# Adaptive average pooling on one core: a partition owns 63 + 1 rows instead of 60 + 4

## The chip, the core and the metric

One core of a Trainium2 chip runs the kernel. The metric is the device time of one execution in microseconds (us); lower is better. The runs before the change took 333.34, 333.5 and 333.92 us, median 333.5.

## The reference

The input has 32 x 256 rows of 4096 float32 numbers, and each row is averaged in 256 windows of 16 neighbours:

```python
def reference(x, output_size):            # x: (32, 256, 4096) float32, output_size 256
    batch, channels, length = x.shape
    result = np.zeros((batch, channels, output_size), dtype=np.float32)
    for i in range(output_size):
        start = int(i * length / output_size)
        end = int((i + 1) * length / output_size)
        result[:, :, i] = np.mean(x[:, :, start:end], axis=-1)
    return result
```

134.22 MB are read and 8.39 MB written. A row is 16 KB of input and 1 KB of output, and there are 8192 rows, 64 for each of the 128 partitions.

## The kernel before

**Who owns which rows.** A tile is four rows for each partition, 64 KB of input per partition, and there are 16 tiles. The first 15 tiles come from one block: partition p owns the 60 neighbouring rows 60p to 60p+59, and tile t takes four of them. In DRAM the neighbouring partitions of such a tile read 960 KB apart. The last tile takes the last 512 rows of the input, four neighbouring rows for each partition, so its partitions read 64 KB apart.

**One tile.** SyncE issues the load of the tile into one of two buffers of the pool `inpool` (L75). The windows of a tile are split in two halves. On the second half GpSimd (POOL, L78) adds the upper eight elements of every window onto the lower eight. Meanwhile VectorE (DVE, L83) sums the windows of the first half, 16 elements each; then it sums the second half's eight (L86), which waits for GpSimd. ScalarE (ACT, L89) multiplies the results by 1/16 in place. The results of the first 15 tiles lie in `res_many`, 60 KB per partition, those of the last in `res_last`, 4 KB.

**Order.** The two buffers set the order: the load of tile t+2 is issued when VectorE has finished with tile t (L86), while the load of tile t+1 is moving. Before the second load VectorE writes 1536 zeros into its buffer (L74), and the load waits for that. All loads and stores are issued by SyncE, in program order, on one DMA queue.

**Stores.** The store of `res_many` stands right behind the last load in SyncE's program (L58 is the helper `store`). It waits until ScalarE has finished the fifteenth tile. When the last tile is done, two more stores follow, split by partition:

```python
    for lo, hi in ((0, 120), (120, P)):
        store(o_last[lo:hi, :], res_last[lo:hi, :])
```

The three stores count on one semaphore of their own, and SyncE waits for all of them at the end.

Of the kernel before, what the change touches and what calls it, by code (L numbers as in the profile page):

```python
# [1 line left out]

# [4 lines left out]


@with_exitstack
def kernel(  # L10
    ctx: ExitStack,
    tc: tile.TileContext,
    x: bass.AP,
    output_size: int,
    out: bass.AP,
):

    nc = tc.nc
    F32 = mybir.dt.float32
    X = mybir.AxisListType.X

    batch, channels, length = x.shape
    ob, oc, olen = out.shape
    assert ob == batch and oc == channels and olen == output_size
    assert length % output_size == 0
    window = length // output_size  # L30
    hw = window // 2
    inv_w = 1.0 / float(window)

    P = nc.NUM_PARTITIONS
    R = 4
    rows = batch * channels
    assert rows % (P * R) == 0
    ntiles = rows // (P * R)
    many = (ntiles - 1) * R
    cells = R * output_size  # L40
    m = cells // 2
    cols = R * length

    xr = x.rearrange("b c l -> (b c) l")
    orow = out.rearrange("b c o -> (b c) o")
    x_many = xr[0 : P * many, :].rearrange("(p r) l -> p (r l)", p=P, r=many)
    o_many = orow[0 : P * many, :].rearrange("(p r) o -> p (r o)", p=P, r=many)
    x_last = xr[P * many :, :].rearrange("(p r) l -> p (r l)", p=P, r=R)
    o_last = orow[P * many :, :].rearrange("(p r) o -> p (r o)", p=P, r=R)

    res_many = nc.alloc_sbuf_tensor("res_many", [P, (ntiles - 1) * cells], F32, align_bytes=256)
    res_last = nc.alloc_sbuf_tensor("res_last", [P, cells], F32, align_bytes=256)
    inpool = ctx.enter_context(tc.tile_pool(name="inpool", bufs=2))

    stored = nc.alloc_semaphore("stored")

    def store(out, in_):
        ins = nc.sync.dma_start(out=out, in_=in_)  # L58
        tc.no_tile_sem_insts.add(ins.ins.name)
        ins.then_inc(stored, 16)  # L60

    for t in range(ntiles):
        last = t == ntiles - 1
        xbuf = inpool.tile([P, cols + 64], F32, name="xin")
        off = 32 if last else 0
        flat = xbuf[:, off : off + cols]
        xin = flat.rearrange("p (o w) -> p o w", w=window)
        if last:
            res, base, src = res_last, 0, x_last
        else:  # L70
            res, base = res_many, t * cells
            src = x_many[:, t * cols : (t + 1) * cols]
        if t == 1:
            nc.vector.memset(flat[:, 0:1536], 0.0)  # L74
        nc.sync.dma_start(out=flat, in_=src)  # L75
        if last:
            store(o_many, res_many[:, :])
        nc.gpsimd.tensor_add(  # L78
            out=xin[:, m:cells, 0:hw],
            in0=xin[:, m:cells, 0:hw],  # L80
            in1=xin[:, m:cells, hw:window],
        )
        nc.vector.reduce_sum(  # L83
            out=res[:, base : base + m], in_=xin[:, 0:m, :], axis=X
        )
        nc.vector.reduce_sum(  # L86
            out=res[:, base + m : base + cells], in_=xin[:, m:cells, 0:hw], axis=X
        )
        nc.scalar.mul(  # L89
            out=res[:, base : base + cells],  # L90
            in_=res[:, base : base + cells],
            mul=inv_w,
        )
    for lo, hi in ((0, 120), (120, P)):
        store(o_last[lo:hi, :], res_last[lo:hi, :])

    ctx.pop_all().close()
    tc.close()
    tc.compile()  # L99
    nc.sync.wait_ge(stored, 48)  # L100
    nc.sync.sem_clear(stored)


# [1 line left out]
_INS = ['x', 'output_size']  # L105
_OUTS = [((32, 256, 256), 'float32')]

_NUMBERS = {'output_size': 256}


# [26 lines left out]
```

## Time and profile before

| what | us |
|---|---|
| device time, median of three runs (333.34 to 333.92) | 333.5 |
| span of the profiled execution, first to last instruction | 332.3 |
| the difference, time around the span | 1.2 |
| VectorE busy | 211.0 |
| GpSimd busy | 139.7 |
| ScalarE busy | 18.2 |
| one GpSimd addition of a tile (128x4096) | 8.72 |
| one VectorE sum of 16 (128x8192 to 128x512) | 8.69 |
| one VectorE sum of eight (128x4096 to 128x512) | 4.42 |
| one ScalarE multiplication (128x1024) | 1.06 |
| one load, time from landing to landing in the steady part | 19.3 |
| first load issued, landed | 0.74, 22.69 |

The profiled execution is known by its span; the time of the runs is taken without the profiler. A view "windows" cuts the span in stretches and gives for each the busy time of the engines, the share of time that the 16 DMA engines were busy, and the GB/s that they moved. A DMA packet is counted whole in the stretch where it starts, so in stretches shorter than a packet the share can exceed 1. "SPq" is SyncE's queue of instructions: a line with it says how long SyncE waited before it could issue a DMA.

### The profile page before, as it was taken

Reading aid. Unit: us, or ns where it says so; the run is one execution under the profiler, and the core shown is the slowest. Engines: PE = TensorE matmul, PEld = TensorE weight load, DVE = VectorE, ACT = ScalarE, POOL = GpSimd, SP = SyncE. Lnnn points to the kernel's source line nnn. Section 1 sums busy time; section 2 is a strip of 40 time slices with the busy share of each in tenths; the row PEclk is TensorE's granted clock in tenths of the full one; section 3 lists DMA queues with packets and bytes.
Section 4 is the critical chain, followed back from the end, with each engine's and each line's share of the span. In section 5 each row is a group of like instructions: output and inputs, shape, how many; then the busy total and the mean of one; then the engine's idle time right before and its main releaser. Section 6 shows DMA issues by size and latency. Waiting matters only on the chain.

```text
span 332.3 us, 162 instructions
## 1 busy us (share of the span) xinstructions
DVE 211.0 (64%) x33; ACT 18.2 (5%) x17; POOL 139.7 (42%) x20
## 2 busy tenths in 40 slices
DVE  1029396692939669392956939295683929578392
ACT  1000101001010100001010000101000010101001
POOL 0027091642709164370906437090633709063370
DMA  9898999989898999989898998989899898989897
GB/s 379 379 505 379 489 394 442 442 379 505 379 505 379 489 394 394 489 379 505 379 497 387 426 458 379 505 379 505 379 481 402 387 497 379 505 379 505 363 473 300
DMA packets 2599, 142.61 MB, mean 429 GB/s; under 512 B 295, under 2 KB 295, under 8 KB 423
## 3 DMA queue, kind: packets, MB, share of 16 engines
q1 hardware_dynamic: 2599, 142.61, 99.4%
HBM read 134.22 MB, written 8.39 MB: 429 GB/s over the span
## 4 chain that ended last, share of the span: by engine, by line
DMA 65%; POOL 18%; DVE 11%; POOLq 3%; issue 0%; ACT 0%
DMA xin<-in_x_dram 65%; POOL xin L78 18%; DVE res_many L86 9%; POOLq L99 3%; DVE res_last L86 1%; DVE xin L74 0%; ACT res_last L89 0%; POOLq L78 0%
## 5 line engine op out<-in xcount | busy, mean ns | idle before, releaser
L78 POOL TENSOR_TENSOR xin<-xin 128x4096 f32<-128x4096 f32 x16 | 139.5, 8717 | 181.9 <-DMA xin<-in_x_dram 181.9
L83 DVE TENSOR_REDUCE res_many<-xin 128x512 f32<-128x8192 f32 x15 | 130.3, 8686 | 105.0 <-DMA xin<-in_x_dram 105.0
L86 DVE TENSOR_REDUCE res_many<-xin 128x512 f32<-128x4096 f32 x15 | 66.3, 4420 | 2.4 <-POOL xin L78 2.3
L89 ACT ACTIVATE res_many<-res_many 128x1024 f32<-128x1024 f32 x15 | 15.8, 1056 | 289.7 <-DVE res_many L86 289.7
L83 DVE TENSOR_REDUCE res_last<-xin 128x512 f32<-128x8192 f32 x1 | 8.7, 8686 | 6.6 <-DMA xin<-in_x_dram 6.6
L86 DVE TENSOR_REDUCE res_last<-xin 128x512 f32<-128x4096 f32 x1 | 4.4, 4422 | 0.2 <-POOL xin L78 0.2
L89 ACT ACTIVATE res_last<-res_last 128x1024 f32<-128x1024 f32 x1 | 1.1, 1056 | 18.8 <-DVE res_last L86 18.8
L74 DVE MEMSET xin<- 128x1536 f32 x1 | 1.3, 1338 | 1.1 <-PEq L118 1.1
L89 ACT ACT_TABLE_LOAD x1 | 1.3, 1283 | 0.7 <-PEq L118 0.7
L118 POOL MEMSET const-float32-0.0<- 128x1 f32 x1 | 0.1, 98 | 0.2 <-issue 0.2
L118 POOL MEMSET const-bfloat16-1.0<- 128x1 bf16 x1 | 0.1, 101 | 0.0
L118 POOL MEMSET const-uint8-127<- 128x1 uint8 x1 | 0.1, 101 | 0.0
L118 POOL MEMSET const-float32-1.0<- 128x1 f32 x1 | 0.1, 98 | 0.0
## 6 DMA issues: line engine op xcount, KB each, us to landing
out_dram<-res_many SPq DMA_DIRECT2D x1, 7680.0 KB
out_dram<-res_last SPq DMA_DIRECT2D x1, 480.0 KB
xin<-in_x_dram SPq DMA_DIRECT2D x16, 25.3
out_dram<-res_last SPq DMA_DIRECT2D x1, 32.0 KB
```

What stands on the lines that cost most here:

```text
L74: nc.vector.memset(flat[:, 0:1536], 0.0)
L78: nc.gpsimd.tensor_add(out=xin[:, m:cells, 0:hw], in0=xin[:, m:cells, 0:hw], in1=xin[:, m:cells, hw:window],)
L83: nc.vector.reduce_sum(out=res[:, base : base + m], in_=xin[:, 0:m, :], axis=X)
L86: nc.vector.reduce_sum(out=res[:, base + m : base + cells], in_=xin[:, m:cells, 0:hw], axis=X)
L89: nc.scalar.mul(out=res[:, base : base + cells], in_=res[:, base : base + cells], mul=inv_w,)
L99: tc.compile()
L118: nc = _bacc.Bacc("TRN2", target_bir_lowering=False, num_devices=1)
```

## The change

A partition now owns 63 neighbouring rows of the block (rows 63p to 63p+62) and one of the last 128 rows. There are 17 loads: three rows, fifteen times four rows, and one row; the neighbouring partitions of the first 16 loads read 1008 KB apart, those of the last 16 KB apart. The results lie in three tensors: `res_many` (59 rows, 59 KB per partition), `res_late` (the last four of the 63, 4 KB) and `res_last` (one row, 1 KB), and each is stored by one DMA over all 128 partitions; the rows of the first two stores are 63 KB apart in DRAM. The split of the last store in 120 and 8 partitions is gone, and so is an offset of 32 elements that the last tile had in its buffer. The operations on a tile are the same, on three, four or one row. The last two loads are issued ahead of the store of `res_many` in SyncE's program, and that store waits for ScalarE's multiplication of the fifteenth load's tile.

```diff
-    ntiles = rows // (P * R)
-    many = (ntiles - 1) * R
-    cells = R * output_size
-    m = cells // 2
+    many = rows // P - 1
+    counts = [many % R] * (many % R > 0) + [R] * (many // R) + [1]
     cols = R * length
...
-    x_last = xr[P * many :, :].rearrange("(p r) l -> p (r l)", p=P, r=R)
-    o_last = orow[P * many :, :].rearrange("(p r) o -> p (r o)", p=P, r=R)
+    x_last = xr[P * many :, :]
+    o_last = orow[P * many :, :]
 
-    res_many = nc.alloc_sbuf_tensor("res_many", [P, (ntiles - 1) * cells], F32, align_bytes=256)
-    res_last = nc.alloc_sbuf_tensor("res_last", [P, cells], F32, align_bytes=256)
+    early = (many - R) * output_size
+    res_many = nc.alloc_sbuf_tensor("res_many", [P, early], F32, align_bytes=256)
+    res_late = nc.alloc_sbuf_tensor("res_late", [P, R * output_size], F32, align_bytes=256)
+    res_last = nc.alloc_sbuf_tensor("res_last", [P, output_size], F32, align_bytes=256)
...
+    def pooled(xin, res, n):
+        m = n // 2
+        nc.gpsimd.tensor_add(
+            out=xin[:, m:n, 0:hw], in0=xin[:, m:n, 0:hw], in1=xin[:, m:n, hw:window]
+        )
+        nc.vector.reduce_sum(out=res[:, 0:m], in_=xin[:, 0:m, :], axis=X)
+        nc.vector.reduce_sum(out=res[:, m:n], in_=xin[:, m:n, 0:hw], axis=X)
+        nc.scalar.mul(out=res, in_=res, mul=inv_w)
+
+    done = 0
+    todo = []
+    for t, count in enumerate(counts):
+        xbuf = inpool.tile([P, cols], F32, name="xin")
+        flat = xbuf[:, 0 : count * length]
+        n = count * output_size
+        if t == len(counts) - 1:
+            res, src = res_last[:, :], x_last
         else:
-            res, base = res_many, t * cells
-            src = x_many[:, t * cols : (t + 1) * cols]
+            src = x_many[:, done * length : (done + count) * length]
+            base = done * output_size
+            res = res_late[:, :] if base == early else res_many[:, base : base + n]
+        done += count
         if t == 1:
             nc.vector.memset(flat[:, 0:1536], 0.0)
         nc.sync.dma_start(out=flat, in_=src)
-        if last:
-            store(o_many, res_many[:, :])
...
-    for lo, hi in ((0, 120), (120, P)):
-        store(o_last[lo:hi, :], res_last[lo:hi, :])
+        todo.append((flat.rearrange("p (o w) -> p o w", w=window), res, n))
+        if t < len(counts) - 2:
+            pooled(*todo.pop())
+
+    store(o_many[:, 0:early], res_many[:, :])
+    for tile_args in todo:
+        pooled(*tile_args)
+    store(o_many[:, early:], res_late[:, :])
+    store(o_last, res_last[:, :])
```

More of the change, by code (lines that the diff above doesn't have):

```diff
@@ L36 @@
     rows = batch * channels
-    assert rows % (P * R) == 0
-    ntiles = rows // (P * R)
-    many = (ntiles - 1) * R
-    cells = R * output_size
-    m = cells // 2
+    assert rows % P == 0
+    many = rows // P - 1
+    counts = [many % R] * (many % R > 0) + [R] * (many // R) + [1]
     cols = R * length
@@ L60, in store @@
         ins.then_inc(stored, 16)
[L62 to L67, printed above, removed]
-        if last:
-            res, base, src = res_last, 0, x_last
-        else:
-            res, base = res_many, t * cells
-            src = x_many[:, t * cols : (t + 1) * cols]
+    def pooled(xin, res, n):
[14 more added lines that the diff above has]
+            res, src = res_last[:, :], x_last
+        else:
+            src = x_many[:, done * length : (done + count) * length]
+            base = done * output_size
+            res = res_late[:, :] if base == early else res_many[:, base : base + n]
+        done += count
         if t == 1:
@@ L75 @@
         nc.sync.dma_start(out=flat, in_=src)
-        if last:
-            store(o_many, res_many[:, :])
[L78 to L93, printed above, removed]
-    for lo, hi in ((0, 120), (120, P)):
-        store(o_last[lo:hi, :], res_last[lo:hi, :])
+        todo.append((flat.rearrange("p (o w) -> p o w", w=window), res, n))
[6 more added lines that the diff above has]
+    store(o_last, res_last[:, :])
     ctx.pop_all().close()
```

## The prediction

> **What bounds the kernel now.** I read the page's busy shares and chain first, then SyncE's own waits, then windows of the end cut finely enough to see single DMA packets.
>
> ```profile
> DVE 211.0 (64%) x33; ACT 18.2 (5%) x17; POOL 139.7 (42%) x20
> DMA packets 2599, 142.61 MB, mean 429 GB/s; under 512 B 295, under 2 KB 295, under 8 KB 423
> q1 hardware_dynamic: 2599, 142.61, 99.4%
> DMA 65%; POOL 18%; DVE 11%; POOLq 3%; issue 0%; ACT 0%
> ```
>
> The chain gives 29% to POOL and DVE, which looks as if compute shared the path. The queue row says otherwise: the 16 DMA engines are occupied for 99.4% of the span. The chain only alternates because a load is issued when its buffer is free; the load before it is still moving then. The waits and the timeline's last events show that:
>
> ```profile
> SPq L75 <- DVE res_many L86: 185.8, 14, 13.3
> 302.02 4.42 DVE L86 TENSOR_REDUCE res_many<-xin 128x512 f32<-128x4096 f32 x1 [0.17 <-POOL xin L78]
> 307.55 0.35 SPq L58 DMA_DIRECT2D out_dram<-res_many  x1
> 313.02 8.69 DVE L83 TENSOR_REDUCE res_last<-xin 128x512 f32<-128x8192 f32 x1 [6.59 <-DMA xin<-in_x_dram]
> 327.42 0.75 SPq L58 DMA_DIRECT2D out_dram<-res_last  x2
> ```
>
> SyncE waits at most 13.3 us for a buffer after a load has landed, and a load takes 19.3, so each load is issued about 6 us before the queue runs dry. The big store is issued at 307.55, 5.5 us before the last load lands (313.02). What is left is the final store, issued at 327.42. Did the DMA engines wait for it? The windows (us, then busy time of the compute engines, then DMA share, then GB/s; a packet is counted where it starts):
>
> ```profile
> 61.32:273.83 212.51, 144.16 (x22) 11.62 (x11) 95.89 (x11) 1.00 1.00 434
> 316.50:316.90 0.40, 0.40 (x1) 0.00 (x0) 0.40 (x1) 1.00 5.31 2304
> 316.90:317.30 0.40, 0.40 (x1) 0.00 (x0) 0.40 (x1) 1.00 0.35 154
> 327.80:328.20 0.40, 0.00 (x0) 0.00 (x0) 0.00 (x0) 1.00 5.32 2304
> 328.48:328.50 0.02, 0.00 (x0) 0.00 (x0) 0.00 (x0) 1.00 7.08 3072
> 328.50:330.10 1.60, 0.00 (x0) 0.00 (x0) 0.00 (x0) 1.00 0.00 0
> 330.10:330.70 0.60, 0.00 (x0) 0.00 (x0) 0.00 (x0) 1.00 0.74 300
> 330.70:331.60 0.90, 0.00 (x0) 0.00 (x0) 0.00 (x0) 1.00 0.92 378
> 331.60:331.90 0.30, 0.00 (x0) 0.00 (x0) 0.00 (x0) 1.00 0.06 14
> ```
>
> The zero from 328.50 to 330.10 is no idle time. 2304 GB/s over 0.40 us is 15 packets of 60 KB, and 3072 over 0.02 is one more: the last round of the big store, one packet on each of 16 engines. A share of 7.08 x 0.02 x 16 makes that packet 2.27 us long, so the 15 end from 330.07 to 330.47 and the sixteenth at 330.76. The 4 KB packets start from 330.10 on, straight behind; the final store was in the queue in time. Issue to first packet takes about 1 us (the first load is issued at 0.74, its packets start from 1.7), so its issue had some 1.7 us to spare. Loads run at 434 GB/s to the end. The bound is the bytes, and the end is set by whichever DMA engine finishes last.
>
> Two details matter. One engine trails by 0.29 us, already at 316.9 and still at 328.49. And 295 packets under 512 B are completion marks, one per engine used: 17 transfers of 128 partitions give 272, so the two final stores give 23 = 15 + 8. The 120 rows go over 15 engines, eight rows each, and the 8 rows over eight engines. One engine gets no final row. By the trace's packet records, followed end to start, that is the one that trails: nothing follows its packet ending at 330.76.
>
> **The change part by part.** Sums are made against the profiled span, 332.3 us; the median 333.5 lies 1.2 above, carried over unchanged.
>
> *Loads.* 3 + 15x4 + 1 rows are the same 64, 134.22 MB. The first lands 19.3/4 = 4.8 earlier, at 17.9; three quarters of a tile's DVE work (13.1 x 0.75 = 9.8) frees its buffer at 27.7, while the second load moves until 37.2. Later loads keep today's order 4.8 earlier: the fifteenth lands at 288.3 (293.16 now), the sixteenth at 307.7, the one-row load at about 313.0 as now. The one-row load is issued at 288.3 + 13.2 = 301.5, 6 us before it is needed. Gain or loss in the queue: none. The memset before the second load stays as it is. Each engine handles 8 more load packets (48 + 16 KB for one 64 KB). A packet's fixed part comes from the windows: 60 KB take 2.27 us, 37.8 ns per KB; 83 packets of 4 KB (378 GB/s x 0.90 us) at a share of 0.92 x 0.90 x 16 = 13.2 us take 160 ns each, 9 ns above 4 x 37.8. So 8 x 0.009 = 0.07 us, at most 0.2 at three times that.
>
> *Compute of the tail.* The last full tile is done at 307.7 + 13.2 + 1.1 = 322.0, and the 4 KB store is issued then. The one-row tile has a quarter of each row's time: POOL 2.2, DVE 2.2 + 1.1, ACT about 0.3. DVE takes it up at 320.9, so the 1 KB store is issued near 324.6. The 59 KB store, issued at 288.3 + 14.4 = 302.7, keeps the engines busy until about 330. Shortening the tail's compute therefore buys nothing: it was hidden with 1.7 us to spare and is now with over 4. Were that cover gone, the wait would cost its overrun. The third store adds an issue on SyncE (0.35 us) behind which only the final wait is queued: nothing.
>
> *Stores.* Each engine now writes 8 x 59, 8 x 4 and 8 x 1 KB, the trailing one included. Its end: 330.76, less 8 KB at 37.8 ns (0.30), plus load packets (0.07), plus 8 x 0.160 = 1.28, plus 8 packets of 1 KB. A 1 KB packet is not in the trace: between 38 ns (bytes alone) and 160 (as the 4 KB row), and I take 47, bytes plus the fixed 9, since 4 and 60 KB packets lie on that line: 0.38. Sum 332.19. Today the last data packet starts near 331.70 and ends at 331.86, a single row of the 8-row store. Difference +0.33 us; bounds with 38 and 160 ns +0.25 and +1.23. If no engine trails, the others end at 330.47 - 0.30 + 0.07 + 1.28 + 0.38 = 331.90: +0.04. From last packet to the span's end are 0.4 us in either kernel.
>
> The row speaks for one late engine that today's split relieves. The Trainium skill, page "DMA: Bandwidth & Descriptors", section "Latency and other measured facts", says that DMA engines 7 and 15 are usually slower than the rest, and guesses at a cause in the GpSimd-issued path. The trace agrees with one such engine (0.29 us), not two, on a queue that SyncE issues; with the page's two the end would be the same +0.33, by the later one.
>
> Forecast: 333.5 + 0.33 = 333.8, +0.1%, less than the 0.2% (0.67 us) that a measurement here tells from no change.
>
> **The rivals.** *Small packets cost more (slower).* The 1 KB packets come last on every engine, with nothing behind to hide them. From 90 ns apiece on (8 x 43 ns above my 47 give 0.34) the loss passes 0.2%; at the 4 KB row's 160 ns the time is 334.7. For it: no packet of this size is in the trace, and the rows are 63 KB apart in DRAM instead of contiguous. Against: the straight line from 4 to 60 KB.
>
> *The new pitch slows the loads (slower).* Neighbouring partitions read 1008 KB apart instead of 960. The point of decision is 0.67/16 = 0.04 us per load. If each load were stretched like the slowest row now (19.86 against 19.29), 16 x 0.57 gives 342.6. Against: loads sit at 434 GB/s, 27.1 per engine, the same as the stores (60 KB in 2.27 us), so the engines and not DRAM set it; the last tile, 64 KB apart, ran at 437 GB/s from 293.16 to 307.55. The same page and section report copies losing rate at row pitches of large powers of two (207 GB/s at 512 KiB, 214 when full), cured by 4 KiB of padding; 1008 KB is 16 KB short of 1 MiB, so by that rule the pitch is harmless, and at 512 KiB's loss the estimate would be +10 us. No run here shows such a pitch yet.
>
> *The end gets tighter (faster).* The stretch 293.16 to 313.02 is 0.5 us longer than another load's, with the excess where loads give way to the store. If a 16 KB last packet and a store queued 10 us ahead remove it, and no late engine or single row trails (0.15), the time is 333.5 - 0.55 - 0.15 = 332.8. Against: the store was queued 5.5 us ahead already and the turn happens once in either kernel.
>
> **How the numbers follow.** Forecast 0.57, all of it inside 0.2%. Small packets 0.20; pitch 0.08; the trailing engine, in ordinary runs, over 0.34 us later than in this profile 0.07: slower 0.35. Tighter end 0.08: faster. The range runs from 333.1 (half of the faster case, and the spread of the three times, 333.34 to 333.92) to 335.0 (the 160 ns case and the same spread); outside lie the pitch and the whole of the tighter end.
>
> **What would show it.** After: some 2880 packets (2560 of data, 20 x 16 marks), 434 GB/s in the steady stretch, the three final stores issued near 303, 322 and 325, no gap ahead of the 4 and 1 KB packets, a last round ending near 332.2. A steady rate under 434, a gap ahead of the final packets, or 1 KB packets over 90 ns would make the forecast wrong, each by its own rival; a span under 331.7 would refute the trailing engine.

## The result and the profile after

The changed kernel takes 334.43 us (median of 13 runs, 333.72 to 335.17) against 333.59 (13 runs, 333.34 to 333.92): a ratio of 1.0028, 95% interval 1.0021 to 1.0035. It is slower by 0.84 us (0.28%), where +0.33 us (0.1%) was forecast; the range of its times is 1.45 us wide against 0.58. The profiled execution has a span of 333.1 us against 332.3.

The page of the changed kernel (DMA packets, queue, chain):

```profile
DMA packets 2880, 142.61 MB, mean 428 GB/s; under 512 B 320, under 2 KB 448, under 8 KB 576
q1 hardware_dynamic: 2880, 142.61, 99.3%
DMA 64%; POOL 21%; DVE 11%; DVEq 1%; issue 0%; ACT 0%; POOLq 0%
```

The bytes and the queue's share (99.3% against 99.4%) are as before; the packets are the 2880 that were forecast. The timeline (start, duration, instruction) shows the order of the tail:

```profile
303.68 0.35 SPq L59 DMA_DIRECT2D out_dram<-res_many  x1
308.64 8.69 DVE L68 TENSOR_REDUCE res_late<-xin 128x512 f32<-128x8192 f32 x1 [6.08 <-DMA xin<-in_x_dram]
323.04 0.34 SPq L59 DMA_DIRECT2D out_dram<-res_late  x1
325.71 0.33 SPq L59 DMA_DIRECT2D out_dram<-res_last  x1
```

Everything comes about 1 us later than forecast (302.7, 307.7, 322.0, 324.6), with the distances right. So the late time was there before the tail. The windows of the steady stretch and of the end (us, compute engines, clock, DMA share, GB/s; a packet counts where it starts):

```profile
61.32:273.83 212.51, 143.94 (x23) 11.62 (x11) 95.67 (x12) 1.00 1.00 434
327.60:328.35 0.75, 0.00 (x0) 0.00 (x0) 0.00 (x0) 1.00 2.60 1128
328.35:328.60 0.25, 0.00 (x0) 0.00 (x0) 0.00 (x0) 1.00 0.56 242
328.60:328.90 0.30, 0.00 (x0) 0.00 (x0) 0.00 (x0) 1.00 0.46 201
328.90:329.80 0.90, 0.00 (x0) 0.00 (x0) 0.00 (x0) 1.00 0.00 0
332.10:332.40 0.30, 0.00 (x0) 0.00 (x0) 0.00 (x0) 1.00 0.10 38
332.40:332.70 0.30, 0.00 (x0) 0.00 (x0) 0.00 (x0) 1.00 0.06 20
332.70:333.10 0.40, 0.00 (x0) 0.00 (x0) 0.00 (x0) 1.00 0.00 0
```

The steady rate is the same 434 GB/s. In the last round of the 59 KB store (1128 x 0.75 = 846 KB) 14 engines start their packet before 328.35, one before 328.60 and one after it. From the packet records the last starts at 328.87, 0.96 us behind the median of the sixteen; before it was 328.49 and 0.37. That engine then writes its 4 KB and 1 KB packets alone: from 332.10 on the DMA share is 0.10 and 0.06, which is what one or two engines of sixteen make. The data end at 332.70 against 331.86.

Where does the late engine come from? The start of the span, when each engine takes up its second packet. Before:

```profile
4.70:5.10 0.40, 0.00 (x0) 0.00 (x0) 0.00 (x0) 1.00 4.54 1966
5.10:5.30 0.20, 0.00 (x0) 0.00 (x0) 0.00 (x0) 1.00 1.51 655
5.30:5.50 0.20, 0.00 (x0) 0.00 (x0) 0.00 (x0) 1.00 1.51 655
```

and the changed kernel:

```profile
4.10:4.50 0.40, 0.00 (x0) 0.00 (x0) 0.00 (x0) 1.00 2.05 860
4.50:4.80 0.30, 0.00 (x0) 0.00 (x0) 0.00 (x0) 1.00 2.65 1147
4.80:5.15 0.35, 0.00 (x0) 0.00 (x0) 0.00 (x0) 1.00 0.00 0
5.15:5.30 0.15, 0.00 (x0) 0.00 (x0) 0.00 (x0) 1.00 0.76 328
5.30:5.60 0.30, 0.00 (x0) 0.00 (x0) 0.00 (x0) 1.00 0.38 164
```

Before, 12 + 2 + 2 packets of 64 KB start within 0.8 us. After, 14 packets of 48 KB start by 4.80, then none, then one, then one more at 5.57. The last engine is 1.06 us behind the median after its very first packet. By the packet records two of the sixteen first packets took 3.50 and 3.74 us, where the median took 2.66. On the last four-row load the latest engine is still 0.82 us behind: each engine takes up its next packet as soon as one ends, and a lag once made wears off slowly.

### The profile page after: what moved, and what is told of

It is laid out like the page before. It is cut to its first block, busy times and chain, and to the rows that moved or that the text cites. A ratio compares the mean times of both kernels' runs of the same rounds, so it can differ in the third digit from the quotient of the medians.

```text
span 333.1 us, 169 instructions
## 1 busy us (share of the span) xinstructions
DVE 211.2 (63%) x35; ACT 18.4 (6%) x18; POOL 139.8 (42%) x21
## 2 busy tenths in 40 slices
DMA packets 2880, 142.61 MB, mean 428 GB/s; under 512 B 320, under 2 KB 448, under 8 KB 576
## 3 DMA queue, kind: packets, MB, share of 16 engines
q1 hardware_dynamic: 2880, 142.61, 99.3%
## 4 chain that ended last, share of the span: by engine, by line
DMA 64%; POOL 21%; DVE 11%; DVEq 1%; issue 0%; ACT 0%; POOLq 0%
DMA xin<-in_x_dram 64%; POOL xin L65 21%; DVE res_many L69 9%; DVE res_late L69 1%; DVEq L100 1%; DVE xin L86 0%; DVE res_last L69 0%; ACT res_last L70 0%; POOLq L65 0%
## 5 line engine op out<-in xcount | busy, mean ns | idle before, releaser
L65 POOL TENSOR_TENSOR xin<-xin 128x4096 f32<-128x4096 f32 (+2 forms) x17 | 139.6, 8215 | 179.7 <-DMA xin<-in_x_dram 179.7
L68 DVE TENSOR_REDUCE res_many<-xin 128x512 f32<-128x8192 f32 (+1 forms) x15 | 128.2, 8544 | 104.3 <-DMA xin<-in_x_dram 104.3
L69 DVE TENSOR_REDUCE res_many<-xin 128x512 f32<-128x4096 f32 (+1 forms) x15 | 65.2, 4349 | 2.4 <-POOL xin L65 2.3
L70 ACT ACTIVATE res_many<-res_many 128x1024 f32<-128x1024 f32 (+1 forms) x15 | 15.6, 1042 | 286.0 <-DVE res_many L69 286.0
L68 DVE TENSOR_REDUCE res_late<-xin 128x512 f32<-128x8192 f32 x1 | 8.7, 8686 | 6.1 <-DMA xin<-in_x_dram 6.1
L69 DVE TENSOR_REDUCE res_late<-xin 128x512 f32<-128x4096 f32 x1 | 4.4, 4421 | 0.2 <-POOL xin L65 0.2
L68 DVE TENSOR_REDUCE res_last<-xin 128x128 f32<-128x2048 f32 x1 | 2.3, 2278 | 0.0
L70 ACT ACTIVATE res_late<-res_late 128x1024 f32<-128x1024 f32 x1 | 1.1, 1057 | 18.3 <-DVE res_late L69 18.3
L69 DVE TENSOR_REDUCE res_last<-xin 128x128 f32<-128x1024 f32 x1 | 1.2, 1210 | 0.0
## 6 DMA issues: line engine op xcount, KB each, us to landing
xin<-in_x_dram SPq DMA_DIRECT2D x1, 6144.0 KB, 17.9
```

The source lines that it names most:

```text
L65: nc.gpsimd.tensor_add(out=xin[:, m:n, 0:hw], in0=xin[:, m:n, 0:hw], in1=xin[:, m:n, hw:window])
L68: nc.vector.reduce_sum(out=res[:, 0:m], in_=xin[:, 0:m, :], axis=X)
L69: nc.vector.reduce_sum(out=res[:, m:n], in_=xin[:, m:n, 0:hw], axis=X)
L70: nc.scalar.mul(out=res, in_=res, mul=inv_w)
```

## The experiments

Two questions were put. First: is one fixed engine always the late one, so that the 120/8 split, which spares it, matters (theory A), or does something make the engines trail further (B)? Then: is it the distance between the partitions' rows in the first load, the "pitch" (C), or something else in the changed kernel (D)? "Lag" is how long the latest of the sixteen engines starts a packet of a round behind the median one, by the packet records; where nothing else is said, it is the lag after the first packet. Of the edits below, "..." stands for lines that are left out.

**The split, taken out and put in.**

```diff
 # before_whole (against before)
-    for lo, hi in ((0, 120), (120, P)):
-        store(o_last[lo:hi, :], res_last[lo:hi, :])
+    store(o_last[:, :], res_last[:, :])
 ...
 # after_split (against the changed kernel)
-    store(o_many[:, early:], res_late[:, :])
+    for lo, hi in ((0, 120), (120, P)):
+        store(o_many[lo:hi, early:], res_late[lo:hi, :])
 ...
```

> The kernel before with its last store whole (128 partitions of 4 KB in one DMA) in place of 120 + 8. Theory A (one fixed DMA engine is always the late one, and the 120/8 split spares it 8 packets of 4 KB): the late engine now writes its 1.28 us too, and ends at 330.76 + 1.28 = 332.04 where 331.86 was the end, or up to 0.8 us later when it trails as far as in the changed kernel (0.96 us): +0.2 to +0.9 us, and the spread of the times widens from 0.6 to over 1 us. Theory B (the 63-row pitch or the 48 KB first load makes engines trail further, the split matters little): within 0.2 us of before, spread as before.

Measured: 333.48 us, ratio 1.0000 (0.9992 to 1.0009), times 333.38 to 333.85. The latest engine trailed by 0.33 us in the last store round, and the data ended at 331.97 instead of 331.86. That is near the 332.04 of theory A, but 0.11 us later is too little to show in the times.

> The changed kernel with the 4 KB store split in 120 and 8 partitions, as the kernel before had its last one. Theory A: the late engine is spared 1.28 us, the end falls to that of the other engines: -0.6 to -0.9 us, back to 333.6 to 333.8 with the narrow spread of before. Theory B: the late engine is now one and now another of the sixteen, so the gain is small (0 to 0.2 us) and the spread stays over 1 us.

Measured: 334.51 us, ratio to before 1.0028 (1.0016 to 1.0039), as the changed kernel. Windows of its end:

```profile
332.14:332.50 0.36, 0.00 (x0) 0.00 (x0) 0.00 (x0) 1.00 0.09 34
332.50:332.84 0.34, 0.00 (x0) 0.00 (x0) 0.00 (x0) 1.00 0.06 21
```

34 GB/s over 0.36 us is 12 KB, two packets of 4 KB and four of 1 KB by the packet records. The late engine's last 59 KB packet ends at 331.24, and eight 4 KB packets follow it without a gap, the last from 332.33 on: it is not the engine that the split spares. Nor is it in before_3first (below), split included: there the data end 1.25 us behind the latest 60 KB packet, which is eight packets of 4 KB. In the first profile of before the late engine and the spared one were the same; these two profiles show that this is no rule. Theory A falls in both directions.

**The packets of the first load.**

```diff
 # after_43
-    counts = [many % R] * (many % R > 0) + [R] * (many // R) + [1]
+    counts = [R, many % R] + [R] * (many // R - 1) + [1]
 # before_3first: the 60 rows as four loads of three and twelve of four
+    sizes = [3] * 4 + [R] * (ntiles - 4) + [R]
 ...
```

> The changed kernel with its loads in the order four rows, three rows, fourteen times four, one: the first load has 64 KB packets as before. Theory A: no change against the changed kernel (+0.8 us over before). Theory B, in the form that a first load of 48 KB packets spreads the engines: the engines' lag falls to 0.4 us as in the profile of before, and the time to +0.2 to +0.4 us over before. If the pitch of 1008 KB spreads them: no change either.

Measured: 335.99 us, ratio 1.0068 (1.0056 to 1.0081). The lag after the first packet is 0.84 us with 64 KB packets too. The other 1.6 us (335.99 against the changed kernel's 334.43) are a cost of the experiment itself, seen in its timeline and in a window of it (the last line):

```profile
36.58 11.60 SPq L87 DMA_DIRECT2D xin<-in_x_dram  x2
37.88 6.55 DVE L68 TENSOR_REDUCE res_many<-xin 128x384 f32<-128x6144 f32 x1 [1.33 <-DMA xin<-in_x_dram]
58.89 8.69 DVE L68 TENSOR_REDUCE res_many<-xin 128x512 f32<-128x8192 f32 x1 [11.07 <-DMA xin<-in_x_dram]
36.00:40.00 4.00, 2.67 (x2) 1.06 (x1) 2.15 (x1) 1.00 0.78 262
```

A three-row load in second place lands at 37.88, the load behind it is issued at 36.58, only 1.3 us ahead, and lands at 58.89: 21.0 us for a load of 19.3. By the packet records its first packets start between 37.54 and 38.28, when the engines have run dry for 1.1 us on average (the DMA share falls to 0.78 in the window), and they take 3.1 us on average where a 64 KB packet usually takes 2.42. The new start spreads the engines anew: the latest ends this packet 0.79 us behind the median. The time of this run says nothing on theory B; its lags do.

> The kernel before (60 + 4 rows, 960 KB pitch, 120/8 split kept) with four loads of three rows first and then twelve of four, and the last as it was. Theory A: within 0.2 us of before, since the split covers whatever the late engine trails. Theory B (48 KB first packets spread the engines): first-round lags near 1 us as in the changed kernel; with the split, a time up to +0.3 us if other engines than the spared one are late.

Measured: 333.57 us, ratio 1.0002 (0.9992 to 1.0011), lag 0.30. Packets of 48 KB at a distance of 960 KB spread the engines no more than those of 64 KB did.

**The distance of the rows, in the first load alone.**

```diff
 # before_t0_63 (against before)
+        if t == 0:
+            src = xr[0 : P * 63, :].rearrange("(p r) l -> p (r l)", p=P, r=63)[:, 0:cols]
 # after_t0_60 (against the changed kernel)
+            if t == 0:
+                src = xr[0 : P * 60, :].rearrange("(p r) l -> p (r l)", p=P, r=60)[:, 0 : count * length]
```

> The changed kernel, except that its first load alone reads rows 60p to 60p+2 (960 KB between partitions), so the first tile's results are of other rows. Theory C: the latest engine trails by 0.3 to 0.4 us, and the time falls to -0.1 to +0.2 us of before, with before's narrow spread. Rival D: lag 0.8 to 1.1 us and +0.8 us, as in the changed kernel.

Measured: 333.53 us, ratio to before 0.9999 (0.9991 to 1.0008), times 333.31 to 333.60. The windows of its second packets:

```profile
4.10:4.50 0.40, 0.00 (x0) 0.00 (x0) 0.00 (x0) 1.00 2.84 1229
4.50:4.80 0.30, 0.00 (x0) 0.00 (x0) 0.00 (x0) 1.00 2.27 983
4.80:5.15 0.35, 0.00 (x0) 0.00 (x0) 0.00 (x0) 1.00 0.00 0
```

and from the timelines the landing of the first load, when VectorE starts on it, here and then in the changed kernel:

```profile
17.73 6.55 DVE L68 TENSOR_REDUCE res_many<-xin 128x384 f32<-128x6144 f32 x1 [15.26 <-DMA xin<-in_x_dram]
```

```profile
18.61 6.55 DVE L68 TENSOR_REDUCE res_many<-xin 128x384 f32<-128x6144 f32 x1 [16.15 <-DMA xin<-in_x_dram]
```

All sixteen start by 4.80 (10 + 6 packets of 48 KB), and the first load lands 0.88 us sooner. One changed address pattern in one load of 17 removes the whole loss, with fifteen loads still at 1008 KB, with the 59, 4 and 1 KB stores and without the split. This decides for C against D.

> The kernel before, except that its first load alone reads rows 63p to 63p+3 (1008 KB between partitions) in place of 60p to 60p+3, so the first tile's results are of other rows; everything else, the 120/8 split too, is before's. Theory C (the engines' first packets, all started within a quarter of a microsecond, come back unevenly when the partitions' rows lie 1008 KB apart; the late engines stay late to the end because the queue never runs empty): after the first packet the latest engine trails the median by 0.8 to 1.1 us (0.4 in before), and the time is +0.4 to +0.9 us over before. Rival D (something else in the changed kernel makes the lag: the sizes of buffers or results in SBUF, or the later loads' pitch): lag 0.3 to 0.4 us, time as before.

Measured: 333.82 us, ratio 1.0011 (1.0003 to 1.0020), lag 0.47: the direction of C, but both the time (+0.3 us) and the lag lie below the ranges that C gave.

**A pitch of 1024 KB.** All 64 rows of a partition from one block:

```diff
+    x_all = xr.rearrange("(p r) l -> p (r l)", p=P, r=many + R)
+    x_many, x_last = x_all[:, 0 : many * length], x_all[:, many * length :]
 ...
```

> The kernel before with all 64 rows of a partition from one block, so that partitions read 1024 KB apart in every load and write 64 KB apart; tiles, order and split are before's. Theory C, if uneven first packets come from pitches near 1 MB: a lag of 1 us or more and +0.5 us or more over before; if engines 4 MB apart kept colliding after the first packet, the steady rate would fall below 434 GB/s too and the time rise by several us. Rival D: as before.

Measured: 356.37 us, ratio 1.0676 (1.0644 to 1.0708). The steady stretch runs at 413 GB/s and not 434:

```profile
61.32:273.83 212.51, 133.04 (x21) 11.62 (x11) 87.17 (x10) 1.00 1.00 413
```

Here the loss doesn't end after the first packets: it goes on through the loads. It isn't C's picture made larger, though. C asked for a lag of 1 us or more after the first packet, and it was 0.45: all sixteen first packets were slow alike (median 3.77 us, against 3.03 in before), and the engines drifted apart later, to 2.30 us of lag on the last load.

**The one-row load first.**

```diff
-    counts = [many % R] * (many % R > 0) + [R] * (many // R) + [1]
+    counts = [1] + [many % R] * (many % R > 0) + [R] * (many // R)
 ...
```

> The changed kernel with its one-row load (rows 16 KB apart) moved from the last place to the first, its 1 KB store issued behind the 59 KB one, and the 4 KB store last. Theory C: the first packets come from rows 16 KB apart; if those come back as evenly as rows 960 KB apart, the lag is 0.3 to 0.4 us and the time within 0.2 us of before; the three-row load behind it starts on engines that are out of step already. Rival D: +0.8 us as the changed kernel. Either way the tail's compute is 14.3 us again behind a last load that lands at 313, so the 4 KB store is issued near 327.4, still ahead of the end of the 59 KB store.

Measured: 333.71 us, ratio 1.0008 (0.9999 to 1.0016), lag 0.25. Rows 16 KB apart in the first load are as good as rows 960 KB apart, and the 63 + 1 layout loses almost nothing when its 1008 KB loads meet engines that are already at work. It is faster than the changed kernel and not faster than before.

**Why only +0.3 with four rows?** Four kernels on one chip, all with 1008 KB in the first load: the changed kernel, the kernel before with a four-row and with a three-row first load of that pitch, and the 63 + 1 layout with a four-row first load.

```diff
 # after_4first: fifteen loads of four rows, then two loads into one buffer
+            nc.sync.dma_start(out=flat[:, 0 : 3 * length], in_=x_three)
+            nc.sync.dma_start(out=flat[:, 3 * length :], in_=x_one)
 # before_3first_t0_63: before_3first, with the first load's rows 63p to 63p+2
```

> The changed kernel once more, beside the three below. Theory C (rows 1008 KB apart make the first packets come back unevenly, and the lag is kept) says nothing against another +0.5 to +0.9 us over before with a spread over 1 us. If the loss hung on the place of the data in DRAM of one run, it could be anything from 0 to +1.

> The kernel before with the first load alone reading rows 63p to 63p+3, once more: +0.3 us again if the four-row first load of that pitch is a milder case than the changed kernel's three-row one; +0.8 us if the first value was the luck of its runs.

> The kernel before with four loads of three rows first, of which the first alone reads rows 63p to 63p+2 (1008 KB apart); its first tile is of other rows. Theory C1 (the pitch matters and 48 KB first packets make it worse): +0.6 to +0.9 us. Theory C2 (the pitch of the first load alone decides, whatever the packets' size): +0.3 us as with four rows. Theory C3 (the first load's pitch is only part, the later loads of the same pitch keep the late engines late): +0.3 us or less.

> 63 + 1 rows with 64 KB packets in the first load: fifteen loads of four rows, then three rows of the block and the one row of the last 128 as two loads into one buffer; stores of 60, 3 and 1 KB per partition; every load but the one-row one reads at 1008 KB. C1: +0.3 us, as the four-row first load at that pitch in the kernel before. C2: +0.3 us. C3: +0.6 to +0.9 us, as the changed kernel.

Measured, in that order: 334.42 us, ratio 1.0028 (1.0019 to 1.0037); 333.98, 1.0017 (1.0009 to 1.0026); 334.43, 1.0022 (1.0012 to 1.0032); 334.05, 1.0018 (1.0009 to 1.0027). All four lose against before. The medians order by packet size in both layouts (+0.9 with 48 KB, +0.45 to +0.5 with 64 KB, and +0.3 in the first run of before_t0_63), as C1 says, against C2 and C3; but the intervals overlap, and after_43 had a lag of 0.84 with 64 KB, so the packet size is a tendency and not shown. In the second run of before_t0_63 the profile caught a heavy case:

```profile
4.70:5.40 0.70, 0.00 (x0) 0.00 (x0) 0.00 (x0) 1.00 3.03 1311
5.40:5.80 0.40, 0.00 (x0) 0.00 (x0) 0.00 (x0) 1.00 0.00 0
5.80:6.30 0.50, 0.00 (x0) 0.00 (x0) 0.00 (x0) 1.00 0.30 131
6.30:6.50 0.20, 0.00 (x0) 0.00 (x0) 0.00 (x0) 1.00 0.76 328
```

14 engines start by 5.40, one more by 6.30 and one at 6.38, 1.22 us behind the median; this execution's span is 333.6 us. From the packet records of one profile each (two where "again" or a second figure stands), beside all times:

| kernel | first load: distance, packet | lag after first packet | lag in last big store round | data end | times, us |
|---|---|---|---|---|---|
| before | 960 KB, 64 KB | 0.38 | 0.37 | 331.86 | 333.34 to 333.92 |
| before_3first | 960 KB, 48 KB | 0.30 | 0.30 | 331.89 | 333.38 to 333.83 |
| after_t0_60 | 960 KB, 48 KB | 0.20 | 0.41 | 331.91 | 333.31 to 333.60 |
| after_1first | 16 KB, 16 KB | 0.25 | 0.40 | 331.92 | 333.56 to 333.93 |
| before_t0_63 | 1008 KB, 64 KB | 0.47, again 1.22 | 0.45, 1.85 | 332.10, 333.17 | 333.58 to 334.87 |
| after_4first | 1008 KB, 64 KB | 0.58 | 0.61 | 332.18 | 333.80 to 334.49 |
| before_3first_t0_63 | 1008 KB, 48 KB | 0.80 | 0.57 | 332.33 | 333.70 to 334.82 |
| changed kernel | 1008 KB, 48 KB | 1.06, again 1.23 | 0.96, 2.01 | 332.70, 333.69 | 333.72 to 335.37 |

The end of the data follows the lag of the last round, and every kernel of the table with 1008 KB in its first load has a higher median than the others. Their times also range wider, over 1.1 to 1.65 us in three of the four; after_4first (0.69) is hardly wider than before (0.58), and the first eleven runs of before_t0_63 alone (0.43) were not.

## Why the prediction was right or wrong

**The number.** The direction was right, the size too small: +0.84 us came for +0.33. That 334.43 lies inside the stated range is in part luck. The range reached up to 335.0 for 1 KB packets of 160 ns, which did not come, and 0.57 of the chances stood on a change inside 0.2%, where 0.28% (0.21% to 0.35%) was measured.

**The bound.** Right: DMA engines busy throughout, steady rate 434 GB/s in both kernels, and the end set by whichever engine finishes last.

**Loads.** Right in the steady stretch, wrong at its start. The first load was taken to land a quarter of a tile earlier, at 17.9; it landed at 18.61, and all that hangs on it moved with it.

**Compute of the tail.** Right: the 4 and 1 KB stores were issued at 323.04 and 325.71, their packets came straight behind the 59 KB ones, and there was no gap.

**Stores.** The 1 KB packet took 46 ns by the packet records, 47 was forecast; so the rival that small packets cost more falls. The late engine's 4 and 1 KB packets took from 331.10 to 332.70, 1.60 us, where 1.28 + 0.38 = 1.66 was summed.

**The failed term** is the late engine's start into the sum of the stores: 330.76 - 0.30 + 0.07 = 330.53 was forecast for the end of its big packets, and it was 331.10. These 0.57 us, less the 0.06 above, are what the end of the data (332.70) lies behind the forecast 332.19. The lag was taken over from the profile of before as a property of one engine that the split spares. Neither holds: the split is worth nothing measurable (before_whole 1.0000), and the late engine of after_split still has its 4 KB packets to write. The lag is made at the start by the first packets, and how large it gets depends on the rows that they read (after_t0_60).

**The rivals.** The pitch rival had the right cause and the wrong place. It looked for a lower steady rate, and 0.04 us per load as its point of decision; there is no such loss, but 0.9 us in the first load. What came true is the case that got 0.07, a trailing engine over 0.34 us later than in the first profile; it was thought of as chance between runs, and is the pitch. The tighter end did not come. From the last four-row load to the last round of the big store the lag grew, from 0.82 to 0.96 us in the changed kernel's profile and from 1.27 to 2.01 in its repeat; in before_3first_t0_63 it stayed (0.59 and 0.57).

By the Trainium skill, page "DMA: Bandwidth & Descriptors", section "Latency and other measured facts", a pad of a few KiB away from a large power of two restores the full rate, which would make 1008 KB harmless. The steady rate agrees (434 GB/s); of the first packets after a start, where this case lost, that row says nothing. Its direction for powers of two is confirmed at a distance that its row doesn't list: 1024 KB, 413 GB/s and 1.0676 in time.

What stays open is why rows 1008 KB apart bring some of the sixteen first packets late, and whether their closeness to 1024 KB is the reason: no other distance near it was tried. That the engines start together, meet at the same part of DRAM and then fall out of step would fit that only the first load suffers, but it is argued and not shown. In the changed kernel's profile the first packets start within 0.26 us; in its repeat they start within 0.65 us, with a larger lag. At 1024 KB the first packets were slow alike and the loss went on behind them, which this picture alone doesn't explain.

## What to carry to other kernels

While the DMA queue never ran empty here, an engine that fell far behind on its first packet stayed behind to the last byte (1.06 us became 0.96), so the address pattern of the first load can cost more than one gains by shortening the tail's compute. Look at a bound of "all engines busy" per engine, not in the mean: cut windows of one packet's length at the start and at the end, and count who starts late. And price a new row distance before using it, in the first load by itself: 1008 KB there cost +0.3 to +0.9 us against 960, and 1024 KB in all loads +23 us.

## What the runs showed of the hardware that was not expected

A distance of 1024 KB between neighbouring partitions slows this load stream by 5% (413 against 434 GB/s) and the kernel by 6.8%, one of 1008 KB only the first packets. A load issued 1.3 us before the one ahead of it has landed isn't early enough: in after_43 it landed 21.0 us after its predecessor instead of 19.3, since its packets started 0.96 us after the issue, on engines that had run dry, and were slow like those of a first load.
